# Pooling differences and low parts of weights spread over three stages of a decoder block, their loads held in place on the DMA queue

## The chip, the cores and the metric

The kernel runs on one core of one Trainium2 chip. The metric is the device time of one execution in microseconds (us). A core has five engines that work side by side: PE multiplies matrices (PEld are its weight loads), DVE and ACT work on whole tiles of 128 partitions, POOL too but only on SBUF, and SP here only issues DMAs. Each engine works off its instructions in an order fixed when the kernel is built; an instruction that waits holds back all behind it on its engine.

## The reference

One decoder block in float32, sequence and model width 1024, batch 1:

```python
h = rms_norm(x, norm_gain) * (1.0 + scale) + shift        # scale, shift, gate from silu(c) @ w_ada + b_ada
q, k, v, z_a, u, z_b, m_a, m_b = split(h @ w_in)          # eight parts of 1024 columns
attn = stick_breaking_attention(q, k, v)                  # 16 heads of 64
p_a = (attn * silu(z_a)) @ w_branch_a
pooled = multiscale_causal_pool(u, pool_w, pool_scale)
p_b = (pooled * silu(z_b)) @ w_branch_b
out = (sigmoid(m_a) * p_a + sigmoid(m_b) * p_b) @ w_out
return rms_norm(x + gate * out, final_gain)
```

The pooling has four groups of 256 channels with windows 2, 4, 8 and 16. For each group it takes the mean over the trailing window minus the token itself (the "difference"), maps it with a 256 x 256 matrix of the group, and scales each channel.

## The kernel before

To keep float32 accuracy, every operand of a large product is held as two halves: a high half (the value rounded to the type that PE takes) and a low half (the value minus the high half). A product is three matmuls: high by high, high by low, low by high. A weight tile is 128 x 1024 (512 KB). A step that projects with one tile has 2 x 24 = 48 matmuls of 512 columns. `split` makes the halves with a cast on one engine and a subtraction on another.

The work goes in stages, in this order of the program:

- u stage: h is made, and u = h @ w_in's part is written to DRAM (`u_d`), the last tiles in the loop `for i in reversed(range(KB))`.
- V stage (`with pool("vp")`): 16 steps of 24 matmuls; ACT and DVE make both halves of each output `vo`, and SP stores them to `v_d`.
- pooling stage (first half of `with pool("pb")`): for each of the four groups two differences are made from u on DVE (L384 to L399), the group's matrix is loaded and split (`praw`, `phl`), and for each of two steps j a projection with a `wzb` tile (48 matmuls) goes through silu into two tiles `zs`; then 12 pooling matmuls read the differences' halves `dhl`, and the scaled product goes to `gb` in halves.
- pb stage: eight steps of 48 matmuls multiply `gb` by `w_branch_b`; `gacc` and `bg` gather the gate.
- attention with the remaining projections ("p"), then the two last products and the norm.

The attention stage needs the low halves of 40 weight tiles. Eight it makes itself. The other 32 ("lows") are made ahead by `make_lo`: load a tile on SP (L134), cast on ACT (L136), subtract on DVE (L137), store to `wl_d` on SP (L138). Calls of it stand in the u stage (8), in V (`LO_V`, 14) and in pb (`LO_PB`, 10).

What sets the order: a planner orders the instructions of each engine when the kernel is built, by the order of the program and by when it expects their inputs and buffers. A DMA that has its buffer may be put far ahead of its place in the program. `tc.keep_in_program_order(ins)` ties an instruction behind the one traced before it on its engine; before the change that is used for loads of the first stage, and for PE's order there and in attention. Buffers with one tag are shared: weight tiles have two raw buffers (`raw`) and two of halves (`whl`), PE's outputs of projections have two banks (`pj`), those of pooling two (`tr`).

Of the kernel before, what the change touches and what calls it, by code (L numbers as in the profile page):

```python
# [9 lines left out]
F32 = mybir.dt.float32  # L10
F32R = mybir.dt.float32r
AF = mybir.ActivationFunctionType
ALU = mybir.AluOpType
PSUM = bass.MemoryType.PSUM

P = 128
D = 1024
S = 1024
# [16 lines left out]


PLAIN = 8
LO_V = (1, 1, 1, 1, 1, 1, 1, 0)
LO_PB = (1, 1, 1, 1, 1, 1, 2, 2)
HD = 64  # L40
BUSY = (10, 2, 2, 2, 6, 2, 0, 2)
EPS = 1e-6
WINDOWS = (2, 4, 8, 16)
# [5 lines left out]
def block_kernel(ctx, tc, a, out):  # L49
    nc = tc.nc  # L50
    v, act, gp = nc.vector, nc.scalar, nc.gpsimd

    def pool(name, **kw):
        return tc.tile_pool(name=name, bufs=1, reuse_waits="tile", **kw)
# [58 lines left out]
        else:  # L113
            v.tensor_copy(dst, src)

    def load_w(src, name, hi_eng, lo_eng):
        raw = wts.tile([P, KB, P], F32, tag="raw", bufs=2, name=name + "_raw")
        nc.sync.dma_start(raw.rearrange("p k c -> p (k c)"), src)
        return split(raw, [P, KB, P], wts, "whl", 2, hi_eng, lo_eng, name)


# [7 lines left out]
    def make_lo(pl, n):  # L129

        for _ in range(n):
            i = next(early_lo)
            raw = pl.tile([P, D], F32, tag="lraw", bufs=3, name=f"l{i}_raw")
            nc.sync.dma_start(raw, a["w_in"][tiles[i]])  # L134
            hi = pl.tile([P, D], F32R, tag="lhi", bufs=1, name=f"l{i}_hi")
            act.copy(hi, raw)  # L136
            v.tensor_sub(raw.bitcast(F32R), raw, hi.bitcast(F32))  # L137
            nc.sync.dma_start(wl_d[i], raw)  # L138

    def load_parts(i, name):  # L140
# [22 lines left out]
    def hmov(sh):  # L163
        return lambda m, kb: m[:, kb, sh * 512:sh * 512 + 512]

    def project(ct, name, use, he, le):
        whl = load_w(a["w_in"][ct], name, he, le)
        for sh in range(2):
            ps = bank("pj", f"{name}_{sh}")
            mm3(ps, whl, (h_hi, h_lo), range(KB), hmov(sh))  # L170
            use(sh, ps)
# [14 lines left out]


    early = ExitStack()
    first = early.enter_context(pool("first"))
    with pool("init") as init:  # L190
        sig = const.tile([P, 8], F32, name="csig")
        act.activation(sig, c_v, AF.Sigmoid)
# [143 lines left out]
            make_h(1, kb, v)  # L336


    with pool("vp") as vp:
        def load_wv(hf, k2):  # L340
            raw = wts.tile([P, 2, 512], F32, tag="raw", bufs=2, name=f"wv{hf}_{k2}_raw")
            nc.sync.dma_start(raw.rearrange("p k c -> p (k c)"), a["w_v"][hf, k2])
            return split(raw, [P, 2, 512], vp, "wv", 6, act, v, f"wv{hf}_{k2}")

        wv = [[load_wv(0, k2) for k2 in range(4)]]
        for i in reversed(range(KB)):
            ps = bank("pj", f"u{i}_1")
            mm3(ps, whl[i], h, range(KB), hmov(1))
            use[i](1, ps)
            make_lo(vp, 1)  # L350
        for hf in range(2):
            if hf == 0:
                wv.append([load_wv(1, k2) for k2 in range(4)])
            for sb in range(8):
                ss = slice(sb * P, (sb + 1) * P)
                ps = bank("pj", f"v{sb}_{hf}")
                for kb in range(KB):
                    hh, hl = h_hi[:, kb, ss], h_lo[:, kb, ss]
                    wh, wl = (w[:, kb % 2] for w in wv[hf][kb // 2])
                    for n, (l, w) in enumerate(((hh, wh), (hh, wl), (hl, wh))):  # L360
                        mm(ps, l, w, start=kb == 0 and n == 0, stop=kb == KB - 1 and n == 2)

                vo = vp.tile([P, 8, 2, HD], F32R, tag="vo", bufs=3, name=f"vo{sb}_{hf}")
                pv = ps.rearrange("p (h d) -> p h d", d=HD)
                act.copy(vo[:, :, 0], pv)
                v.tensor_sub(vo[:, :, 1], pv, vo[:, :, 0].bitcast(F32))
                nc.sync.dma_start(
                    v_d[4 * hf:4 * hf + 4, :, sb].rearrange("n p c -> p n c"),
                    vo.rearrange("p (n h) i d -> p n (h i d)", h=2).bitcast(F32),
                )  # L370
                make_lo(vp, LO_V[sb])
    early.close()


    with pool("pb") as pb:
        invn = pb.tile([P, 16], F32, name="invn")
        for j in range(16):
            gp.memset(invn[:, j:j + 1], 1.0 / (16 - j))
        gb = pb.tile([P, 2, KB, S], F32R, name="gb")
        for g, win in enumerate(WINDOWS):  # L380
            dhl = []
            for cb in range(2):
                j = 2 * g + cb
                u = pb.tile([P, S + 16], F32, tag="u", bufs=2, name=f"u{j}")  # L384
                v.memset(u[:, S:], 0.0)
                nc.sync.dma_start(u[:, :S], u_d[j])
                cur, n, step = u, S + 16, 1
                while step < win:
                    nxt = pb.tile([P, S + 16], F32, tag="win", bufs=2, name=f"win{j}_{step}")
                    n -= step  # L390
                    v.tensor_add(nxt[:, :n], cur[:, :n], cur[:, step:step + n])  # L391
                    cur, step = nxt, 2 * step
                t0 = S - win + 1
                d = pb.tile([P, S], F32, tag="win", bufs=2, name=f"d{j}")
                v.scalar_tensor_tensor(d[:, :t0], cur[:, :t0], 1.0 / win, u[:, :t0], ALU.mult, ALU.subtract)
                tl = pb.tile([P, 16], F32, tag="tl", bufs=2, name=f"tl{j}")
                v.tensor_mul(tl[:, :win - 1], cur[:, t0:S], invn[:, 16 - win + 1:])
                v.tensor_sub(d[:, t0:], tl[:, :win - 1], u[:, t0:S])
                dhl.append(split(d, [P, S], pb, "dhl", 3, v, v, f"dhl{j}"))  # L399
            praw = wts.tile([P, 2, 256], F32, tag="raw", bufs=2, name=f"praw{g}")  # L400
            nc.sync.dma_start(praw, a["pool_w"][g].rearrange("(k p) d -> p k d", p=P))
            ph, pl_ = split(praw, [P, 2, 256], pb, "phl", 1, v, v, f"phl{g}")
            for ob in range(2):
                j = 2 * g + ob
                zs = [pb.tile([P, 512], F32, tag="zs", bufs=3, name=f"zs{j}_{sh}") for sh in range(2)]

                def silu(sh, ps):
                    act.activation(zs[sh], ps, AF.Sigmoid)
                    v.tensor_mul(zs[sh], ps, zs[sh])  # L409

                project(CZB + j, f"wzb{j}", silu, v, gp)
                for sh in range(2):
                    sl = slice(sh * 512, sh * 512 + 512)
                    ps = bank("tr", f"pool{j}_{sh}")
                    for cb in range(2):
                        (dh, dl) = dhl[cb]
                        oc = slice(ob * P, ob * P + P)
                        for i, (w, m) in enumerate(((ph, dh), (ph, dl), (pl_, dh))):
                            mm(ps, w[:, cb, oc], m[:, sl], start=cb == 0 and i == 0, stop=cb == 1 and i == 2)
                    z = zs[sh]  # L420
                    v.scalar_tensor_tensor(z, ps, psc_v[:, j:j + 1], z, ALU.mult, ALU.mult)
                    act.copy(gb[:, 0, j, sl], z)
                    v.tensor_sub(gb[:, 1, j, sl], z, gb[:, 0, j, sl].bitcast(F32))
        gacc, bg = (pb.tile([P, S + 16], F32, tag="u", bufs=2, name=n)[:, :D] for n in ("gacc", "bg"))
        nc.sync.dma_start(bg, a["b_gate"].broadcast_to([P, D]))
        for j in range(KB):
            sm = [pb.tile([P, 512], F32, tag="zs", bufs=3, name=f"sm{j}_{sh}") for sh in range(2)]
            whl = load_w(a["w_branch_b"][j], f"wb{j}", v, gp)
            wg = wts.tile([P, D], F32, tag="raw", bufs=2, name=f"wg{j}")
            nc.sync.dma_start(wg, a["w_gate"][j * P:(j + 1) * P, :])  # L430
            if j == 0:
                v.tensor_scalar_mul(gacc, wg, sc[:, 0:1])
            else:
                v.scalar_tensor_tensor(gacc, wg, sc[:, j:j + 1], gacc, ALU.mult, ALU.add)
            for sh in range(2):
                ps = bank("pj", f"pb{j}_{sh}")
                mm3(ps, whl, (gb[:, 0], gb[:, 1]), range(KB), hmov(sh))
                act.copy(sm[sh], ps)
                nc.sync.dma_start(pb_d[j][:, sh * 512:sh * 512 + 512], sm[sh])
            make_lo(pb, LO_PB[j])  # L440

        for hf in range(2):
            sl = slice(hf * 512, hf * 512 + 512)
            ps = bank("z", f"gate{hf}")
            mm(ps, ones, gacc[:, sl], start=True, stop=True)
            v.tensor_add(bg[:, sl], ps, bg[:, sl])
        nc.sync.dma_start(g_d, bg[0:1, :])


    logits = ExitStack()  # L450
# [388 lines left out]
```

## Time and profile before

| what | value |
|---|---|
| median of 3 runs | 1255.46 us (1254.77 to 1256.27) |
| the profiled execution: own time, span | 1254.13 us, 1252.4 us |
| mean granted clock of PE | 0.991 |
| busy over the span: PE, DVE, ACT, POOL | 97%, 65%, 44%, 18% |
| PE's u products end, V's end, pooling's end, pb's end | 120.5, 207.6, 326.9, 414.8 us |

The profiled execution was recorded by the hardware profiler; its times are counted from the span's start. A granted clock of 1 is PE's full speed of 2.4 GHz, 0.5 is 1.2 GHz, and means of a stretch lie between.

### The profile page before, as it was taken

The page shows a single profiled execution, that of the slowest core. Times are in us where ns is not written, and L with a number is a line of the kernel's source. Part 1 is how long each engine was busy: PE and PEld are TensorE (multiplying, and loading weights), DVE is VectorE, ACT ScalarE, POOL GpSimd, SP SyncE. Part 2 cuts the span into 40 slices and gives each one's busy share as a digit, 9 for nine tenths or more (in the row PEclk, how much of TensorE's full clock was granted, in tenths as well). Part 3 has the DMA queues.
Part 4 walks back from the last instruction along what each step waited for, and adds up shares of the span by engine and source line. Part 5 has one row for each costly group of instructions (what it writes and reads, how often), then busy time and mean ns, then how long its engine had stood idle before and what let it go on. Part 6 is the DMA issues. An engine that isn't in the chain of part 4 may idle for free.

```text
span 1252.4 us, 16055 instructions
## 1 busy us (share of the span) xinstructions
PE 1217.4 (97%) x5744; PEld 1006.5 (80%) x5744; DVE 810.9 (65%) x1081; ACT 547.6 (44%) x1026; POOL 226.1 (18%) x373
## 2 busy tenths in 40 slices
PE   5999999899999999999999999999999999899997
PEld 4888888688888888888888888888888888688886
DVE  7633452999411178786878878687787854675653
ACT  4654331321101265565656556566665644331101
POOL 2100010111222342222323122222212310000001
PEclk9999999999999999999999999999999999899999
DMA  9658994753333411233323224231233246964512
GB/s 351 237 181 329 347 351 176 269 177 102 118 136 133 152 47 51 72 125 103 125 70 114 84 97 126 93 124 59 87 118 102 93 132 220 358 214 151 194 59 85
DMA packets 72946, 192.97 MB, mean 154 GB/s; under 512 B 7713, under 2 KB 21025, under 8 KB 70946
## 3 DMA queue, kind: packets, MB, share of 16 engines
q1 hardware_dynamic: 62098, 172.80, 39.9%
q10 hardware_dynamic: 10768, 19.14, 4.6%
q8 instruction: 45, 0.74, 0.2%
q14 instruction: 35, 0.29, 0.1%
HBM read 137.38 MB, written 50.34 MB: 150 GB/s over the span
## 4 chain that ended last, share of the span: by engine, by line
PE 71%; issue 10%; DVE 10%; DMA 4%; POOL 2%; ACT 1%; SPq 0%; POOLq 0%; DVEq 0%; ACTq 0%
PE p L90 24%; PE pb L90 7%; PE v L90 7%; PE pa L90 7%; PE o L90 6%; PE u L90 4%; PE z L90 4%; PE av L90 4%; PE wt L90 4%; PE ua L90 2%; DMA l_raw<-in_w_in 1%; DVE om L579 1%; DVE be L580 1%; DVE win L391 1%; POOL om L577 1%
## 5 line engine op out<-in xcount | busy, mean ns | idle before, releaser
L90 PE MATMUL p<-hT,w 128*128 128x512 f32 x1920 | 534.5, 399 | 0.0
L90 PEld LDWEIGHTS p<-hT,w 128*128 128x128 f32 x1920 | 341.5, 188 | 56.7 <-issue 0.5
L579 DVE TENSOR_TENSOR_SCAN om<-om 128x512 f32<-128x512 f32 (+7 forms) x128 | 175.2, 1368 | 51.8 <-POOL om L577 28.3
L572 ACT ACTIVATE om<-z 128x512 f32<-128x512 f32 (+2 forms) x192 | 94.3, 491 | 103.9 <-PE z L90 101.9
L599 DVE TENSOR_TENSOR wt<-wt,wt 128x512 fp32r<-128x512 f32 (+1 forms) x160 | 101.0, 632 | 47.5 <-ACT wt L598 46.2
L577 POOL TENSOR_SCALAR_AFFINE_SELECT om<-om 128x128 f32<-128x128 f32 x128 | 65.8, 514 | 328.3 <-ACT om L572 301.9
L598 ACT CAST wt<-wt 128x512 fp32r<-128x512 f32 (+1 forms) x160 | 87.3, 546 | 68.7 <-PE wt L90 64.6
L580 DVE TENSOR_TENSOR be<-be,om 128x511 f32<-128x511 f32 (+7 forms) x128 | 99.7, 779 | 10.5
L90 PE MATMUL pa<-ga,wa 128*128 128x512 f32 x384 | 92.6, 399 | 4.7 <-ACT m_sg L176 4.7
L90 PE MATMUL av<-wt,vv 128*128 128x512 f32 x320 | 94.4, 376 | 0.0
L90 PEld LDWEIGHTS wt<-ident,be 128*128 128x128 f32 x576 | 72.1, 140 | 27.5 <-DVE wt L599 3.2
L573 ACT ACTIVATE be<-z 128x512 f32<-128x512 f32 (+2 forms) x192 | 93.6, 488 | 0.0
L90 PE MATMUL wt<-ident,be 128*128 128x128 f32 x576 | 89.2, 273 | 3.8 <-DVE wt L599 3.8
L90 PE MATMUL wzb<-hT,wzb 128*128 128x512 f32 x384 | 91.9, 394 | 0.1
L90 PEld LDWEIGHTS pa<-ga,wa 128*128 128x128 f32 x384 | 73.5, 192 | 21.6 <-ACT m_sg L176 5.1
L90 PE MATMUL o<-wo,mhl 128*128 128x512 f32 (+1 forms) x408 | 89.8, 377 | 0.0
L90 PE MATMUL pb<-gb,wb 128*128 128x512 f32 x384 | 88.1, 391 | 0.0
L90 PE MATMUL v<-wv,hT 128*128 128x512 f32 x384 | 87.2, 389 | 0.0
L90 PEld LDWEIGHTS wzb<-hT,wzb 128*128 128x128 f32 x384 | 73.0, 190 | 16.5 <-DVE zs L409 0.7
L90 PEld LDWEIGHTS o<-wo,mhl 128*128 128x128 f32 x408 | 73.5, 188 | 14.4
L90 PEld LDWEIGHTS pb<-gb,wb 128*128 128x128 f32 x384 | 72.1, 188 | 15.8
L90 PEld LDWEIGHTS v<-wv,hT 128*128 128x128 f32 x384 | 72.1, 188 | 14.9
(119 smaller groups left out, 1461.9 us busy)
## 6 DMA issues: line engine op xcount, KB each, us to landing
w_raw<-in_w_in SPq DMA_DIRECT2D x40, 512.0 KB, 4.4
l_raw<-in_w_in SPq DMA_DIRECT2D x32, 512.0 KB, 5.5
wl_d<-l_raw SPq DMA_DIRECT2D x32, 512.0 KB, 5.1
w<-wl_d SPq DMA_DIRECT2D x32, 512.0 KB, 3.7
v_d<-vo SPq DMA_DIRECT2D x16, 512.0 KB, 5.2
vv<-v_d SPq DMA_DIRECT2D x8, 1024.0 KB, 5.9
wa_raw<-in_w_branch_a SPq DMA_DIRECT2D x16, 512.0 KB, 4.5
wa<-in_w_mod SPq DMA_DIRECT2D x7, 1024.0 KB, 7.9
```

Of the source, the lines that this page charges most:

```text
L90: ins = op(*args, **kw)
L391: v.tensor_add(nxt[:, :n], cur[:, :n], cur[:, step:step + n])
L572: act.activation(om[:, b0:b0 + n], zp[:, :n], AF.Sigmoid, scale=-0.125)
L573: act.activation(be[:, b0:b0 + n], zp[:, :n], AF.Sigmoid, scale=0.125)
L577: gp.affine_select(out=tl[:, :P], in_=tl[:, :P], pattern=[[1, P]], compare_op=ALU.is_gt, fill=fill, base=0, channel_multiplier=-1)
L579: v.tensor_tensor_scan(om[:, :W], om[:, :W], om[:, :W], 1.0, ALU.mult, ALU.min)
L580: v.tensor_mul(be[:, 1:W], be[:, 1:W], om[:, :W - 1])
L598: act.copy(wt[:, 0, :off], pt[:, :off])
L599: v.tensor_sub(wt[:, 1, :off], pt[:, :off], wt[:, 0, :off].bitcast(F32))
```

## The change

Three differences (tiles 0, 1 and 2) are made in the V stage, after its steps 1, 5 and 10 (counted from 0); the other five in the pooling stage, after the projections of steps 0, 2, 3, 4 and 5. The lows are spread: 8 in the u stage, 6 in V, 10 in pooling, 8 in pb. Loads of u, of lows and of the first `wzb` tile (now traced in V, behind step 13) are held behind the DMA traced before them on SP (`load_behind`). The halves of `wzb` are made by ACT and DVE instead of DVE and POOL. A low is cast and subtracted in two pieces of 512 columns with one buffer for the high half, and there are two raw buffers for lows instead of three. `zs` has two buffers instead of three, `dhl` four instead of three. The tiles of the first stage, and later those of the differences, lie on the right side of the memory; `gacc` and `bg` have places of their own; the small constants `invn` are set earlier.

```diff
-LO_V = (1, 1, 1, 1, 1, 1, 1, 0)
-LO_PB = (1, 1, 1, 1, 1, 1, 2, 2)
+LO_V = (0, 1, 0, 1, 0, 1, 0, 0)
+LO_PB = (1, 1, 1, 1, 1, 1, 1, 1)
+DIFFS = {1: 0, 5: 1, 10: 2}
+DIFFS_POOL = {0: 3, 2: 4, 3: 5, 4: 6, 5: 7}
+LO_POOL = (1, 1, 1, 1, 1, 1, 2, 2)
...
+    def load_behind(dst, src):
+        tc.keep_in_program_order(nc.sync.dma_start(dst, src))
...
-            raw = pl.tile([P, D], F32, tag="lraw", bufs=3, name=f"l{i}_raw")
-            nc.sync.dma_start(raw, a["w_in"][tiles[i]])
-            hi = pl.tile([P, D], F32R, tag="lhi", bufs=1, name=f"l{i}_hi")
-            act.copy(hi, raw)
-            v.tensor_sub(raw.bitcast(F32R), raw, hi.bitcast(F32))
+            raw = pl.tile([P, D], F32, tag="lraw", bufs=2, name=f"l{i}_raw")
+            load_behind(raw, a["w_in"][tiles[i]])
+            for hf in range(2):
+                part = raw[:, hf * 512:hf * 512 + 512]
+                hi = pl.tile([P, 512], F32R, tag="lhi", bufs=1, name=f"l{i}_hi{hf}")
+                act.copy(hi, part)
+                v.tensor_sub(part.bitcast(F32R), part, hi.bitcast(F32))
             nc.sync.dma_start(wl_d[i], raw)
...
-    first = early.enter_context(pool("first"))
+    first = early.enter_context(pool("first", side="right"))
...
+    def make_d(j):
+        win = WINDOWS[j // 2]
+        u = dif.tile([P, S + 16], F32, tag="u", bufs=2, name=f"u{j}")
+        v.memset(u[:, S:], 0.0)
+        load_behind(u[:, :S], u_d[j])
+        cur, n, step = u, S + 16, 1
+        while step < win:
+            nxt = dif.tile([P, S + 16], F32, tag="win", bufs=2, name=f"win{j}_{step}")
+            n -= step
+            v.tensor_add(nxt[:, :n], cur[:, :n], cur[:, step:step + n])
+            cur, step = nxt, 2 * step
+        t0 = S - win + 1
+        d = dif.tile([P, S], F32, tag="win", bufs=2, name=f"d{j}")
+        v.scalar_tensor_tensor(d[:, :t0], cur[:, :t0], 1.0 / win, u[:, :t0], ALU.mult, ALU.subtract)
+        tl = dif.tile([P, 16], F32, tag="tl", bufs=2, name=f"tl{j}")
+        v.tensor_mul(tl[:, :win - 1], cur[:, t0:S], invn[:, 16 - win + 1:])
+        v.tensor_sub(d[:, t0:], tl[:, :win - 1], u[:, t0:S])
+        dhls[j] = split(d, [P, S], dif, "dhl", 4, v, v, f"dhl{j}")
...
-                make_lo(vp, LO_V[sb])
-    early.close()
+                make_lo(lo, LO_V[sb])
+                if 8 * hf + sb == 13:
+                    wzb0 = load_w(a["w_in"][CZB], "wzb0", act, v, True)
+                if 8 * hf + sb in DIFFS:
+                    make_d(DIFFS[8 * hf + sb])
...
-                zs = [pb.tile([P, 512], F32, tag="zs", bufs=3, name=f"zs{j}_{sh}") for sh in range(2)]
+                zs = [pb.tile([P, 512], F32, tag="zs", bufs=2, name=f"zs{j}_{sh}") for sh in range(2)]
...
-                project(CZB + j, f"wzb{j}", silu, v, gp)
+                project(CZB + j, f"wzb{j}", silu, act, v, wzb0 if j == 0 else None)
+                if j in DIFFS_POOL:
+                    make_d(DIFFS_POOL[j])
...
+                make_lo(lo, LO_POOL[j])
+        diffs.close()
+        late = ctx_pb.enter_context(pool("late", side="right"))
+        gacc, bg = (late.tile([P, D], F32, name=n) for n in ("gacc", "bg"))
...
-            make_lo(pb, LO_PB[j])
+            make_lo(lo, LO_PB[j])
```

## Rows read from the trace of the kernel before

**Rows 1.** The page's first part: engine, busy us (share of span), instructions.

```profile
PE 1217.4 (97%) x5744; PEld 1006.5 (80%) x5744; DVE 810.9 (65%) x1081; ACT 547.6 (44%) x1026; POOL 226.1 (18%) x373
```

**Rows 2.** Windows: stretch, its length, busy us (instructions) by engine, clock, DMA share, GB/s.

```profile
core 0: us, PE busy (x) PEld busy (x) DVE busy (x) ACT busy (x) POOL busy (x), PEclk, DMA share, GB/s
120.50:207.60 87.10, 87.10 (x386) 72.14 (x385) 32.95 (x34) 26.97 (x34) 5.26 (x18) 1.00 0.81 287
207.60:326.90 119.30, 113.59 (x481) 92.07 (x480) 109.72 (x142) 28.57 (x41) 19.78 (x8) 0.97 0.55 185
220.00:240.00 20.00, 17.65 (x78) 14.13 (x76) 19.93 (x23) 4.72 (x5) 5.67 (x2) 1.00 0.81 275
240.00:260.00 20.00, 16.74 (x58) 13.09 (x59) 20.00 (x29) 8.17 (x11) 1.41 (x1) 0.83 0.73 239
280.00:300.00 20.00, 20.00 (x89) 16.45 (x88) 19.83 (x27) 3.04 (x5) 2.40 (x1) 1.00 0.30 106
326.90:414.80 87.90, 87.90 (x385) 72.11 (x384) 14.25 (x15) 11.02 (x18) 18.09 (x8) 1.00 0.37 129
```

**Rows 3.** PE's timeline in the pooling stage: start, us, form, count, idle before and releaser.

```profile
235.65 2.01 PE L90 MATMUL wzb<-hT,wzb 128*128 128x512 f32 x8
240.44 4.60 PE L90 MATMUL pool<-dhl,phl 128*128 128x512 f32 x12 [2.79 <-DVE u L385]
247.86 1.15 PE L90 MATMUL pool<-dhl,phl 128*128 128x512 f32 x2 [2.82 <-DVE phl L114]
...
271.27 2.89 PE L90 MATMUL pool<-dhl,phl 128*128 128x512 f32 x12
```

**Rows 4.** The chain of waits: start, us, what.

```profile
120.52 87.05 PE v L90 x384
```

**Rows 5.** DVE's groups in the pooling stage: busy, mean ns of one, idle before.

```profile
L105 DVE TENSOR_TENSOR dhl<-d,dhl 128x1024 fp32r<-128x1024 f32 x8 | 15.3, 1909 | 0.0
L137 DVE TENSOR_TENSOR l_raw<-l_raw,l_hi 128x1024 fp32r<-128x1024 f32 x10 | 12.1, 1214 | 0.8 <-ACT l_hi L136 0.8
...
L391 DVE TENSOR_TENSOR win<-win 128x1037 f32<-128x1037 f32 x6 | 10.2, 1700 | 0.1
L391 DVE TENSOR_TENSOR win<-u 128x1039 f32<-128x1039 f32 x8 | 9.9, 1234 | 0.1
...
L395 DVE SCALAR_TENSOR_TENSOR d<-win,u 128x1021 f32<-128x1021 f32 x2 | 4.7, 2325 | 0.0
L114 DVE CAST wzb<-wzb_raw 128x1024 fp32r<-128x1024 f32 x6 | 4.1, 685 | 0.0
```

**Rows 6.** POOL's groups in the pooling stage.

```profile
L105 POOL TENSOR_TENSOR wzb<-wzb_raw,wzb 128x1024 fp32r<-128x1024 f32 x6 | 16.2, 2696 | 103.7 <-DVE wzb L114 103.7
```

**Rows 7.** ACT's and DVE's groups in the V stage.

```profile
L136 ACT CAST l_hi<-l_raw 128x1024 fp32r<-128x1024 f32 x15 | 15.8, 1051 | 21.4 <-DMA l_raw<-in_w_in 18.5 <-DVE l_raw L137 1.3 <-DVE vo L366 1.2
L366 DVE TENSOR_TENSOR vo<-v,vo 128x512 fp32r<-128x512 f32 x15 | 10.3, 689 | 22.1 <-ACT vo L365 20.4 <-DMA praw<-in_pool_w 1.7
L365 ACT CAST vo<-v 128x512 fp32r<-128x512 f32 x16 | 9.4, 587 | 37.6 <-PE v L90 35.0 <-DMA l_raw<-in_w_in 2.6
...
L110 ACT CAST wv<-wv_raw 128x1024 fp32r<-128x1024 f32 x2 | 2.1, 1054 | 1.1 <-PE v L90 1.1
```

**Rows 8.** The timeline around V's end.

```profile
197.33 0.69 DVE L366 TENSOR_TENSOR vo<-v,vo 128x512 fp32r<-128x512 f32 x1 [4.75 <-ACT vo L365]
...
207.39 16.25 PE L90 MATMUL wzb<-hT,wzb 128*128 128x512 f32 x71
```

**Rows 9.** DMA issues from 60 to 420 us: count, KB each, median us to landing.

```profile
l_raw<-in_w_in SPq DMA_DIRECT2D x32, 512.0 KB, 5.5
...
wb_raw<-in_w_branch_b SPq DMA_DIRECT2D x8, 512.0 KB, 3.4
```

**Rows 10.** What SP's queue waited for: us in total, times, longest.

```profile
SPq L138 <- DVE l_raw L137: 46.2, 27, 3.8
```

More of the change, by code (lines that the diff above doesn't have):

```diff
@@ L114, in copy_to, with load_w @@
             v.tensor_copy(dst, src)
-    def load_w(src, name, hi_eng, lo_eng):
+    def load_behind(dst, src):
+        tc.keep_in_program_order(nc.sync.dma_start(dst, src))
+    def load_w(src, name, hi_eng, lo_eng, behind=False):
         raw = wts.tile([P, KB, P], F32, tag="raw", bufs=2, name=name + "_raw")
-        nc.sync.dma_start(raw.rearrange("p k c -> p (k c)"), src)
+        (load_behind if behind else nc.sync.dma_start)(raw.rearrange("p k c -> p (k c)"), src)
         return split(raw, [P, KB, P], wts, "whl", 2, hi_eng, lo_eng, name)
@@ L164, in hmov, with project @@
         return lambda m, kb: m[:, kb, sh * 512:sh * 512 + 512]
-    def project(ct, name, use, he, le):
-        whl = load_w(a["w_in"][ct], name, he, le)
+    def project(ct, name, use, he, le, whl=None):
+        if whl is None:
+            whl = load_w(a["w_in"][ct], name, he, le)
         for sh in range(2):
@@ L336, in block_kernel @@
             make_h(1, kb, v)
+    invn = const.tile([P, 16], F32, name="invn")
+    for j in range(16):
+        gp.memset(invn[:, j:j + 1], 1.0 / (16 - j))
+    dhls = {}
+    def make_d(j):
[16 more added lines that the diff above has]
+        dhls[j] = split(d, [P, S], dif, "dhl", 4, v, v, f"dhl{j}")
+    lows = ExitStack()
+    lo = lows.enter_context(pool("lo"))
     with pool("vp") as vp:
@@ L349, in block_kernel @@
             use[i](1, ps)
-            make_lo(vp, 1)
+            make_lo(lo, 1)
+        early.close()
+        diffs = ExitStack()
+        dif = diffs.enter_context(pool("dif", side="right"))
         for hf in range(2):
@@ L370, in block_kernel @@
                 )
-                make_lo(vp, LO_V[sb])
-    early.close()
[L375 to L378, printed above, removed]
+                make_lo(lo, LO_V[sb])
[3 more added lines that the diff above has]
+                    make_d(DIFFS[8 * hf + sb])
+    with ExitStack() as ctx_pb:
+        pb = ctx_pb.enter_context(pool("pb"))
         gb = pb.tile([P, 2, KB, S], F32R, name="gb")
         for g, win in enumerate(WINDOWS):
[L381 to L399, printed above, removed]
+            dhl = [dhls[2 * g], dhls[2 * g + 1]]
             praw = wts.tile([P, 2, 256], F32, tag="raw", bufs=2, name=f"praw{g}")
@@ L423, in block_kernel @@
                     v.tensor_sub(gb[:, 1, j, sl], z, gb[:, 0, j, sl].bitcast(F32))
-        gacc, bg = (pb.tile([P, S + 16], F32, tag="u", bufs=2, name=n)[:, :D] for n in ("gacc", "bg"))
+                make_lo(lo, LO_POOL[j])
+        diffs.close()
+        late = ctx_pb.enter_context(pool("late", side="right"))
+        gacc, bg = (late.tile([P, D], F32, name=n) for n in ("gacc", "bg"))
         nc.sync.dma_start(bg, a["b_gate"].broadcast_to([P, D]))
         for j in range(KB):
-            sm = [pb.tile([P, 512], F32, tag="zs", bufs=3, name=f"sm{j}_{sh}") for sh in range(2)]
+            sm = [pb.tile([P, 512], F32, tag="zs", bufs=2, name=f"sm{j}_{sh}") for sh in range(2)]
             whl = load_w(a["w_branch_b"][j], f"wb{j}", v, gp)
@@ L447, in block_kernel @@
         nc.sync.dma_start(g_d, bg[0:1, :])
+    lows.close()
     logits = ExitStack()
```

## Prediction

> **What bounds the kernel now.** The engine table at the head of the profile comes first: PE is busy for 97% of the span [rows 1], so a change on other engines pays only where PE waits or runs slowly. The windows by stage show where that is [rows 2]. In the V stage PE is busy for all of its 87.10 us. In the pooling stage (207.6 to 326.9 us) it is busy for 113.59 of 119.30 us, and DVE for 109.72, which makes DVE the suspect. Between 220 and 260 us DVE has no free time, PE is idle for 2.35 and 3.26 us and the granted clock of the second half falls to 0.83; from 280 to 300 DVE is as full (19.83 of 20) and PE has no idle time at all. So DVE's load alone is not fatal: what hurts is that too much comes at the start.
>
> The PE timeline shows the two stops [rows 3]: the pooling matmuls at 240.44 and 247.86 us wait for DVE, first for a chain that makes a difference, then for the halves of the pooling weights. After the first stop twelve pooling matmuls take 4.60 us; later twelve take 2.89.
>
> How much is there to win? The chain of waits has V's 384 matmuls in 87.05 us, 0.2267 us each [rows 4]. The pooling stage has 480 of the same length, 108.8 us, and lasts 119.3: 10.5 us are lost. Idle time is 5.7 of it, the slow clock most of the rest. The Trainium skill (Perfetto Trace Analysis, Identifying the Most-Contended Engine) says that busy time of matmuls is a bad measure of the distance to the roofline and that busy time of weight loads is a good one. By that measure the stage holds 92.07 us of weight loads where V holds 72.14 in 87.10 [rows 2], which would be 111.2 us of full speed and only 8.1 us to win. I keep the count, since a weight load's busy time does not separate fast and slow clock; the lower cap appears below as a rival.
>
> **The change part by part.** *Three differences go to V.* One costs DVE log2(window) additions of a whole tile, one scaled subtraction, one cast and one subtraction for the halves. A whole-tile operation of two inputs takes 1.23, a cast 0.69 [rows 5]. With windows 2, 2 and 4 that is 4.4 + 4.4 + 5.6 = 14.4 us off the pooling stage (the tails of at most 15 elements left out). V's DVE has room: 32.95 busy of 87.10, and it loses lows too (22 before V's end in the program, now 14). Their three loads of u come on SP; cost nothing, hidden by V's matmuls. If one lands late, DVE stands in front of V's output copies; that belongs to the rival on the other side.
>
> *POOL leaves the wzb halves.* POOL subtracted six tiles in this stage at 2.70 us each [rows 6]. In the same stretch some DVE operations are stretched: the means 1.909, 1.700 and 2.325 of three groups stand against 1.234 of the clean one [rows 5]. The excess is 8 x 0.675 + 6 x 0.466 + 2 x 1.09 = 10.4 us, which I take as returned. The casts go to ACT, 4.1 us off DVE; eight subtractions come on, 8 x 1.23 = 9.8. ACT takes 8 x 1.05 = 8.4 [rows 7] on top of 28.57 of 119.3.
>
> *Lows.* Before, those of the pb stage were free to load early, and ten of them ran in the pooling stage: 12.1 us of DVE [rows 5]. Now ten belong there, spread over eight steps, and eight follow in pb, where DVE is busy for 14.25 of 87.90 [rows 2]. In halves one costs 2 x 0.69 [rows 7] rather than 1.21: 1.6 more for ten. In pb, POOL still splits wb and may stretch their subtractions; 14.25 of 87.90 hides that. With one buffer for the high half, ACT and DVE alternate, which makes the latency 2 x (0.59 + 0.69) = 2.55 us.
>
> DVE's sum for the stage: 109.7 - 14.4 - 10.4 - 4.1 + 9.8 + 1.6 = 92.2 us in some 110. That is 84%, under the 99% at which PE had no idle time between 280 and 300. So most of the 10.5 us should come free. For stops that remain I take 1.0 us; the bounds are none and the 5.7 of now.
>
> *The new wait at the boundary.* Every held load stands behind the DMA traced before it on SP. In the thirteenth V step this makes one line: store of V's output, load of a low, its halves, store of the low, and only behind that store the load of wzb0. That step's DVE subtraction starts at 197.33 and ends at 198.02 [rows 8]. From there: landing of the low, halves 2.55, landing of wzb0, cast 1.05, subtraction 1.21 [rows 7, 5]. A load of that size lands in 3.4 us where the queue is quiet and in 5.5 where it is full [rows 9]. So both halves of wzb0 are there at 198.0 + 3.4 + 2.55 + 3.4 + 1.05 + 1.21 = 209.6 at best and at 213.8 at worst, and PE leaves V at 207.4 [rows 8], where it goes straight into 71 wzb matmuls now. The new stop is 2.2 to 6.4 us long. Behind that low's store SP also holds the loads of the pooling weights, so PE has little else to do. I take 3.0, near the quiet end, since little else moves then. After it the clock is slow, as after the stop at 240 us: 4.60 - 2.89 = 1.7 us.
>
> *The rest costs nothing.* Two zs buffers instead of three: a step has 48 wzb matmuls, 10.9 us, between one use and the next, against some 3 us of ACT and DVE. Two raw buffers for lows: the loads are paced now anyway. The other side of the memory, gacc and bg with places of their own, POOL's small memsets earlier: all are far from their use; without that cover each costs an operation of at most 1.2 us.
>
> Sum: 10.5 - 3.0 - 1.7 - 1.0 = 4.8 us less. Against the profiled execution's own 1254.13 that is 1249.3; the median of the runs shown, 1255.46, is 1.3 higher, which makes 1250.6, rounded to 1250.5.
>
> **The rivals.** *The boundary is hidden.* If PE finds the pooling matmuls or the next wzb at 207 us, 3.0 + 1.7 stay saved: a gain of 9.5, 1246.0. For it: DMAs that are not held run ahead, as the ten lows did. Against it: tiles behind wzb0 share its two raw buffers and two buffers of halves, and its step is first.
>
> *Nothing measurable.* At the busy landing the stop is 6.4 and 1.7 of clock, and with 1.0 of small stops 1.4 are left: 1254.0. It would end there too if weight loads, not matmuls, set PE's pace in this stage and the rest of its loss stayed. Against the first, SP moves little at V's end; against the second, the count of matmuls. The weight-load measure of the Trainium skill (same page and section) would give 8.1 - 4.7 - 1.0 = 2.4 us of gain, an estimate of 1253.1.
>
> *Slower.* A low's store on SP waits for DVE [rows 10], and the next held load now waits behind that store. In the u stage eight lows thus become one line of landing plus 2.55 each. ACT and DVE work in a fixed order; if that order counts on 3.4 us and landings take 5.5, each low is 2.1 later than its place, eight of them 16.8. The copies of u and V queued behind a waiting cast on ACT free PE's two banks, and PE stops when they are more than one step of 24 matmuls late, 5.4 us. So from the third low on it costs, at most 16.8 - 5.4 = 11.4 us; less the gain of 4.8 this is 6.6 slower, 1262.1. For it: in V ACT waited 18.5 us for landings of lows [rows 7], with three buffers. Against it: PE lost nothing in V then, the queue was fuller, and V's lows now start anew behind each store.
>
> **How the numbers follow.** The forecast gets 0.55, the hidden boundary 0.13, nothing measurable 0.18 (0.15 for late landings, 0.03 for the smaller cap), slower 0.14. The range from 1245.5 to 1258.0 takes in the first three with their bounds and the milder part of the fourth; the forecast's own range is 1247.5 to 1253.0. A difference under 0.2%, 2.5 us, is about what a measurement of this kernel cannot tell from no change. Faster by more: 0.13 and 0.51 of the forecast's 0.55, so 0.64; the same: 0.18 and 0.04, less a little for its bad end, 0.21; slower: 0.15.
>
> **What would show it.** Right: DVE under 95 us in the pooling stage, no POOL subtraction in it and no two-input DVE group above 1.3 us; PE without stops at its third step; one stop of about 3 us at V's end that ends with wzb0's halves and is followed by a slow clock; lows in pb. Wrong: PE idle in the u or V stage behind ACT or DVE (slower); wzb or pooling matmuls right at V's end (hidden); DVE still full with PE waiting for dhl.

## The result and the profile after

The changed kernel took 1259.21 us (median of 7 runs, 1256.71 to 1260.89). The kernel before, on the same chip, took 1255.32 (7 runs, 1254.76 to 1256.85). The ratio is 1.0026, 95% interval 1.0016 to 1.0036: slower by 3.9 us where 4.8 less were forecast, and outside the range. The profiled execution took 1258.37 us, 4.2 more than the one before; its span is 1256.4 us, which holds 4.0 of that. The page's engine table of the changed kernel, to be read against [rows 1]:

```profile
PE 1213.0 (97%) x5744; PEld 1004.0 (80%) x5744; DVE 809.6 (64%) x1113; ACT 560.0 (45%) x1066; POOL 205.3 (16%) x365
```

It tells nothing: every share is within two points of what it was. The windows by stage, against [rows 2] (stretch, length, busy us by engine, clock, DMA share, GB/s):

```profile
core 0: us, PE busy (x) PEld busy (x) DVE busy (x) ACT busy (x) POOL busy (x), PEclk, DMA share, GB/s
...
120.50:207.60 87.10, 81.89 (x355) 65.99 (x355) 39.18 (x60) 22.00 (x37) 0.00 (x0) 1.00 0.68 227
207.60:220.00 12.40, 6.75 (x30) 5.26 (x28) 2.77 (x4) 3.20 (x5) 0.00 (x0) 0.93 0.73 224
220.00:240.00 20.00, 19.68 (x77) 16.09 (x78) 16.91 (x23) 7.17 (x11) 0.00 (x0) 0.87 0.76 260
240.00:260.00 20.00, 20.00 (x90) 16.57 (x89) 19.93 (x31) 6.46 (x10) 0.00 (x0) 1.00 0.59 221
...
326.90:414.80 87.90, 87.90 (x389) 72.80 (x389) 26.23 (x33) 19.58 (x33) 19.13 (x8) 1.00 0.64 216
```

From 240 us on the pooling stage is what was promised: PE full at full clock, POOL without a subtraction of `wzb`. But V, which had not one idle PE microsecond before, now has 5.2 in the same 87.10, and in the 12.4 us from 207.6 on, in which V ends, PE is idle nearly half the time. PE's timeline says where (start, us, form, count, idle before and what ended it):

```profile
120.31 21.92 PE L95 MATMUL v<-wv,hT 128*128 128x512 f32 x96
142.43 5.73 PE L95 MATMUL v<-wv,hT 128*128 128x512 f32 x24 [0.19 <-DVE vo L407]
150.77 11.22 PE L95 MATMUL v<-wv,hT 128*128 128x512 f32 x48 [2.60 <-DVE vo L407]
162.79 10.16 PE L95 MATMUL v<-wv,hT 128*128 128x512 f32 x43 [0.81 <-DVE vo L407]
174.18 1.43 PE L95 MATMUL v<-wv,hT 128*128 128x512 f32 x5 [1.23 <-DVE wv L110]
175.99 38.36 PE L95 MATMUL v<-wv,hT 128*128 128x512 f32 x168 [0.38 <-DVE vo L407]
220.31 13.41 PE L95 MATMUL wzb<-hT,wzb 128*128 128x512 f32 x48 [5.97 <-ACT wzb L115]
...
236.28 11.04 PE L95 MATMUL wzb<-hT,wzb 128*128 128x512 f32 x48
```

V stops five times, four of them for `vo`, the copies that free PE's banks. Then comes one stop of 5.97 us for wzb0, and 48 matmuls at 13.41 us instead of 11.04. After that not one stop is left up to the end of pb. The account, from first matmul to first matmul (the timeline for the starts, [rows 3, 4] and the windows for before; the first wzb after 220.31, the first pb matmul at 331.64 in the chain):

| stretch | before | after | difference |
|---|---|---|---|
| V's start | 120.52 | 120.31 | -0.2 |
| V, 384 matmuls | 87.05 | 94.03 | +7.0 (5.2 idle, the rest in the pieces beside the stops) |
| stop at V's end | 0 | 5.97 | +6.0 |
| pooling, 480 matmuls | 119.3 | 111.33 | -8.0 (10.5 regained, 2.5 lost to the slow clock at its start) |
| pb, 384 matmuls | 87.9 | 87.05 | -0.9 |
| sum | | | +3.9 |

The chain of waits from 100 us on shows the cause in V (start, us, what; of its pieces only the loads of lows and one store are shown):

```profile
100.28 6.13 DMA l_raw<-in_w_in
109.61 5.74 DMA l_raw<-in_w_in
118.57 4.63 DMA l_raw<-in_w_in
126.40 4.93 DMA l_raw<-in_w_in
134.54 4.43 DMA l_raw<-in_w_in
142.22 6.47 DMA l_raw<-in_w_in
...
151.52 3.80 DMA wl_d<-l_raw
...
155.34 5.37 DMA l_raw<-in_w_in
```

The lows of the u stage stand in one line, each load behind the store of the low before. The last load shown, at 155.34 us, is that of V's first low; it waited until the store begun at 151.52 had landed, which gave it one of the two raw buffers. The first casts of the eight begin at 95.74, 106.48, 115.43, 123.27, 131.41, 139.05, 148.77 and 157.08 us in the timeline: 8.8 apart in the mean, where a landing of 5.5 and halves of 2.55, the prediction's figures, make 8.05. Before they began between 87.91 and 121.59. How one of them stops PE is seen at the stop of 2.60 us in the timeline of all engines:

```profile
148.77 0.62 ACT L146 CAST l_hi<-l_raw 128x512 fp32r<-128x512 f32 x1 [7.23 <-DMA l_raw<-in_w_in]
149.29 0.58 ACT L406 CAST vo<-v 128x512 fp32r<-128x512 f32 x1
...
150.03 0.68 DVE L407 TENSOR_TENSOR vo<-v,vo 128x512 fp32r<-128x512 f32 x1
...
150.77 1.45 PE L95 MATMUL v<-wv,hT 128*128 128x512 f32 x5 [2.60 <-DVE vo L407]
```

ACT waits 7.23 us with a cast of a low in its hands; the copy of V's finished output stands behind it; PE, which has two banks for its outputs, waits until DVE has taken the rest of it. At V's end the line is the one that was forecast, only longer:

```profile
204.13 0.69 DVE L407 TENSOR_TENSOR vo<-v,vo 128x512 fp32r<-128x512 f32 x1 [0.28 <-ACT vo L406]
...
205.31 1.41 SPq L122 DMA_DIRECT2D l_raw<-in_w_in  x1
...
210.91 0.62 ACT L146 CAST l_hi<-l_raw 128x512 fp32r<-128x512 f32 x1 [1.38 <-DMA l_raw<-in_w_in]
...
213.67 0.32 SPq L148 DMA_DIRECT2D wl_d<-l_raw  x1
214.04 0.42 SPq L122 DMA_DIRECT2D wzb_raw<-in_w_in  x1
...
219.22 1.04 ACT L115 CAST wzb<-wzb_raw 128x1024 fp32r<-128x1024 f32 x1 [4.25 <-DMA wzb_raw<-in_w_in]
```

### The profile page after: what moved, and what is told of

The parts are those of the page before. It is cut to its first block, busy times and chain, and to the rows that moved or that the text cites. A ratio compares the mean times of both kernels' runs of the same rounds, so it can differ in the third digit from the quotient of the medians.

```text
span 1256.4 us, 16108 instructions
## 1 busy us (share of the span) xinstructions
PE 1213.0 (97%) x5744; PEld 1004.0 (80%) x5744; DVE 809.6 (64%) x1113; ACT 560.0 (45%) x1066; POOL 205.3 (16%) x365
## 4 chain that ended last, share of the span: by engine, by line
PE 69%; issue 10%; DMA 7%; DVE 6%; POOL 3%; ACT 2%; SPq 0%; POOLq 0%; DVEq 0%; ACTq 0%
PE p L95 23%; PE wzb L95 7%; PE pb L95 7%; PE pa L95 7%; PE o L95 6%; DMA l_raw<-in_w_in 4%; PE z L95 4%; PE wt L95 4%; PE av L95 4%; PE ua L95 2%; PE v L95 2%; PE pool L95 2%; DVE om L609 2%; DVE be L610 2%; PE u L95 1%
## 5 line engine op out<-in xcount | busy, mean ns | idle before, releaser
L147 DVE TENSOR_TENSOR l_raw<-l_raw,l_hi 128x512 fp32r<-128x512 f32 x64 | 44.1, 689 | 112.2 <-ACT l_hi L146 112.1
L146 ACT CAST l_hi<-l_raw 128x512 fp32r<-128x512 f32 x64 | 39.8, 621 | 129.2 <-DMA l_raw<-in_w_in 107.7
L95 PE MATMUL av<-wt,vv 128*128 128x512 f32 x320 | 94.1, 375 | 0.0
```

Source lines behind the costliest of these rows:

```text
L95: ins = op(*args, **kw)
L146: act.copy(hi, part)
L147: v.tensor_sub(part.bitcast(F32R), part, hi.bitcast(F32))
```

## The experiments

The theory after this result: two lines of held loads lose the time, that of the u stage's lows in V (7.0 us) and that of wzb0 behind a low (6.0 and 2.5 of clock), and the two are separate. The rival: V's stops come from what was moved into V, not from the order of loads.

**Only the u stage's lows set free.** (`make_lo` got a third argument, `held`; with False its load is an ordinary one.)

```diff
-            make_lo(lo, 1)
+            make_lo(lo, 1, False)
```

> The loads of the eight lows of the u stage are not held; everything else is the changed kernel. Theory (the lows of the u stage form one line of landing, halves, store, next load, and ACT's copies of V's outputs stand behind their casts): V takes 87 to 88.5 us again instead of 94.0, the stop at V's end stays at 5 to 6 us with its slow clock, and the time falls by 5 to 7 us to 1252 to 1254. Rival (V's loss comes from the three differences on DVE there): V stays at 92 to 94 us and the time within 2 us of 1259.2.

Measured: 1251.56 us (1250.18 to 1252.81), ratio to the kernel before 0.9965 [0.9952, 0.9978]: 7.7 less than the changed kernel, a little more than expected. V has one stop of 0.83 us left, the boundary keeps its own:

```profile
132.45 76.45 PE L95 MATMUL v<-wv,hT 128*128 128x512 f32 x336 [0.83 <-DVE vo L407]
214.78 12.49 PE L95 MATMUL wzb<-hT,wzb 128*128 128x512 f32 x48 [5.87 <-ACT wzb L115]
```

**Only wzb0 traced ahead of the low of step 13.**

```diff
-                make_lo(lo, LO_V[sb])
                 if 8 * hf + sb == 13:
                     wzb0 = load_w(a["w_in"][CZB], "wzb0", act, v, True)
+                make_lo(lo, LO_V[sb])
```

> The load of the first wzb tile is traced, and held, ahead of the low of V's step 13 instead of behind it. Theory (that low's landing, halves and store make the line at V's end): the first wzb matmul follows V's last within 0.5 us at full clock, 6.0 + 2.5 us saved, 1250 to 1252; V stays at 92 to 94 us. Rival (the two raw buffers or the halves' buffers come free late): a stop of over 3 us stays and the time is above 1255.

Measured: 1250.71 us (1247.86 to 1254.88), 0.9962 [0.995, 0.9974]. The mirror image: no stop at the boundary, and V as long as before (94.1 us), with four of its stops left.

```profile
151.69 22.50 PE L95 MATMUL v<-wv,hT 128*128 128x512 f32 x91 [3.00 <-DVE vo L407]
...
214.38 11.15 PE L95 MATMUL wzb<-hT,wzb 128*128 128x512 f32 x48
```

**Both.**

> Both edits together. Theory: the two losses are apart from each other and add up: V in 87 to 88.5 us, no stop at its end, pooling in 109 to 110, 1243 to 1246, faster than the kernel before. Rival (one loss hides the other, as a late V gives wzb0 its time): 1248 or more.

Measured: 1243.13 us (1243.1 to 1246.4), 0.9904 [0.9888, 0.9921]: 12 us faster than before, 16 faster than the change. The two losses add up (7.7 and 8.5 alone, 16.1 together). The differences are still in V, and V runs without a stop, so what was moved there is not what stopped it. PE's timeline, then the window of the pooling stage:

```profile
120.58 87.20 PE L95 MATMUL v<-wv,hT 128*128 128x512 f32 x384
207.62 11.04 PE L95 MATMUL wzb<-hT,wzb 128*128 128x512 f32 x48
```

```profile
207.60:316.60 109.00, 109.00 (x482) 90.26 (x481) 90.14 (x129) 38.16 (x60) 4.28 (x2) 1.00 0.54 189
```

The pooling stage takes the 108.8 us of its matmuls and no more, with DVE at 90.14.

**Nothing held at all** (base: the changed kernel).

```diff
-        tc.keep_in_program_order(nc.sync.dma_start(dst, src))
+        nc.sync.dma_start(dst, src)
```

> No load of lows, of u or of wzb0 is held; the lists, the places in the program and the split of wzb stay as in the changed kernel. Theory: V keeps its 87 us and wzb0 is there in time, but lows run ahead of their places into V and the start of pooling, so that DVE or DMA stops PE there for 2 to 6 us: 1246 to 1252. Rival (holding is what keeps pooling clean): pooling loses 8 us or more as before the change, 1254 or more.

Measured: 1254.02 us (1250.92 to 1255.77), 0.9981 [0.9971, 0.9992]. Neither expectation holds as a whole: the pooling stage lost 3.2 us (112.0 for its 108.8), as the theory had it, but V, which was to stay clean, took 96.0 us (121.53 to 217.56), with stops for `vo` in other places, the longest

```profile
164.72 23.68 PE L95 MATMUL v<-wv,hT 128*128 128x512 f32 x96 [2.94 <-DVE vo L407]
```

So holding is not the fault as such; some of the held loads protect V. Which ones, the next two tell, on the kernel with both edits (1243.13).

**V's six lows not held.**

```diff
-                make_lo(lo, LO_V[sb])
+                make_lo(lo, LO_V[sb], False)
```

> The kernel with both edits (1243.1), but the six lows of V are not held either; loads of u and of wzb0 stay held, lows of pooling and pb too. Theory (a held low in V starts behind a store that PE paces, so its lateness cannot grow; a free one runs early and puts its casts ahead of V's copies): V 89 to 95 us, 1245 to 1251. Rival (in the run where nothing was held, V lost to the differences, not to the lows): V within 1 us of 87, 1242.5 to 1244.5.

Measured: 1250.7 us (1249.63 to 1252.28), 0.9958 [0.9943, 0.9973]. As the theory had it: V took 94.4 us, so holding V's lows is worth some 7 us. The longest stop:

```profile
151.41 12.78 PE L95 MATMUL v<-wv,hT 128*128 128x512 f32 x48 [3.85 <-DVE vo L407]
```

**The loads of u not held.**

```diff
-        load_behind(u[:, :S], u_d[j])
+        nc.sync.dma_start(u[:, :S], u_d[j])
```

> The kernel with both edits, but the loads of u for all differences are not held; all lows of V, pooling and pb stay held. Theory (the lows make the trouble): V within 2 us of 87 and the time 1243 to 1246. Rival (differences that run early stand on DVE ahead of V's copies): V 90 us or more, 1246 to 1251.

Measured: 1245.42 us (1244.39 to 1245.71), 0.9912 [0.9896, 0.9929]; V 88.7 us with stops of 0.33 and 0.54. The theory's numbers hold. Whether holding these loads is worth anything stays open: the trace is 2.4 us longer than that with both edits, but the ratio's interval overlaps that one's, [0.9888, 0.9921].

**How many held lows does it take in the u stage?** First four of the eight, then two (`make_lo(lo, 1, i >= 4)` and `i >= 6`; the loop counts down).

> Base is the kernel with both edits (1243.1). Here the last four of the eight lows of the u stage are not held and the first four are. Theory (lateness adds up along the line of held lows and PE pays only what exceeds one V step): four held lows are late by some 2 us each, 8 against 5.4 us of slack, so V costs 0 to 3 us and the time is 1243 to 1246. Rival (any held low in the u stage shifts the whole line behind it): V 93 us or more, 1248 to 1251.

Measured: a median of 1247.77 us, 0.993 [0.9912, 0.9949], but the profiled execution was 1243.34 and the others 1247.5 to 1248.4. V took 88.4 us in the trace, which is that of the fastest execution and does not explain the median: undecided.

> The kernel with both edits, but the first two of the u stage's eight lows are held. Theory (lateness adds up along the line, 2 us each, and PE has 5.4 us of slack): V within 1 us of 87, 1243 to 1244.5 in all runs. Rival (any held low there costs): V above 89 us, 1246 or more.

Measured: 1249.62 us (1248.9 to 1252.86), 0.9953 [0.9936, 0.997], and V 94.6. Two held lows cost nearly as much as eight, and PE stops at once:

```profile
127.47 5.74 PE L95 MATMUL v<-wv,hT 128*128 128x512 f32 x24 [1.23 <-ACT u_sg L194]
134.29 5.73 PE L95 MATMUL v<-wv,hT 128*128 128x512 f32 x24 [1.07 <-DVE vo L407]
140.18 16.61 PE L95 MATMUL v<-wv,hT 128*128 128x512 f32 x72 [0.16 <-DVE vo L407]
158.93 56.32 PE L95 MATMUL v<-wv,hT 128*128 128x512 f32 x240 [2.14 <-DVE vo L407]
```

That topples my law of sizes, lateness that adds up low by low until it passes 5.4 us. With both edits the first cast of a low began at 88.11 us, because its load was free to go out early; as soon as the first is held, it stands behind loads of `wv` that wait for buffers, and begins at 95.42. The seven that follow are all later than with both edits, held or not.

**The waiting taken off ACT and DVE.** The kernel with two held lows, but POOL makes the halves of the eight lows of the u stage.

```diff
-                act.copy(hi, part)
-                v.tensor_sub(part.bitcast(F32R), part, hi.bitcast(F32))
+                copy_to(gp if pool_halves else act, hi, part)
+                (gp if pool_halves else v).tensor_tensor(part.bitcast(F32R), part, hi.bitcast(F32), op=ALU.subtract)
...
-            make_lo(lo, 1, i >= 6)
+            make_lo(lo, 1, i >= 6, True)
```

> The kernel with two held lows (1249.62 us, V 94.6 us with stops of 1.23, 1.07, 0.16 and 2.14), but POOL makes the halves of the eight lows of the u stage, so that none of their casts stands on ACT and none of their subtractions on DVE; the loads stay as they were, two of them held. Theory: a held load costs time because a cast or a subtraction that waits for it stands on ACT or DVE ahead of the copies that free PE's banks. Then the three stops before 150 us (2.46 us and the slow clock behind each) go, V takes 87 to 91 us and the time is 1243.5 to 1247; the stop at 158.93, where DVE waited for a load of u, may stay. Rival: the held load costs through SP's queue alone, by making the loads and stores behind it late. Then V stays at 94 or more and the time at 1249 or more, and stops with DVE or ACT as releaser stay before 150 us. Price of POOL: some 1.2 us for each of four operations of a low, so a low takes landing plus about 5 us instead of 2.55, with two buffers; DVE may be stretched beside it, which V's free DVE hides in both theories.

Measured: 1251.81 us (1249.53 to 1252.7), 0.9968 [0.9957, 0.998], V 95.95. The theory's numbers were missed, and by the time and V's length the rival would have it; the place of the stops says otherwise. (The granted clock of the kernel with two held lows is 1.00 from 120.5 to 150 us, so the slow clock that the expectation counted behind the first three stops was not there to be won.) PE's timeline, then what ACT and DVE did (all engines):

```profile
120.22 27.36 PE L95 MATMUL v<-wv,hT 128*128 128x512 f32 x120
154.76 61.57 PE L95 MATMUL v<-wv,hT 128*128 128x512 f32 x264 [7.18 <-DVE vo L407]
```

```profile
143.39 0.62 POOL L117 TENSOR_SCALAR l_hi<-l_raw 128x512 fp32r<-128x512 f32 x1 [3.55 <-DMA l_raw<-in_w_in]
...
151.39 0.62 ACT L115 CAST l_hi<-l_raw 128x512 fp32r<-128x512 f32 x1 [14.06 <-DMA l_raw<-in_w_in]
...
153.29 1.07 ACT L406 CAST vo<-v 128x512 fp32r<-128x512 f32 x2
```

While POOL does the waiting (up to 3.55 us at a time in V) PE runs 120 matmuls without a stop where the kernel with two held lows stopped three times. The first low of V is still on ACT, and its load came out of the same line, which POOL makes longer still, at 147.16 us in the timeline: there ACT waits 14.06 us, two copies of V's output pile up behind it, and PE stops for 7.18. So both halves of the mechanism are seen: the line sets how late a low is, and the lateness cost nothing while POOL did the waiting and 7.18 us where ACT did it with copies behind. Taken off one engine, the loss went to the next low.

The last three look at the side that went well.

**POOL put back on the wzb halves** (on the kernel with both edits).

```diff
-                project(CZB + j, f"wzb{j}", silu, act, v, wzb0 if j == 0 else None)
+                project(CZB + j, f"wzb{j}", silu, v, gp, wzb0 if j == 0 else None)
```

(and wzb0's halves likewise)

> The kernel with both edits, but the halves of wzb are made by DVE (cast) and POOL (subtraction) again. Theory (DVE has room once differences and lows are spread): DVE's groups are stretched by some 10 us in sum, its busy time in pooling rises from about 90 to about 96 us, PE loses 0 to 2 us: 1243 to 1245.5. Rival (POOL leaving wzb is what freed pooling): PE waits for DVE in pooling as before, 3 us or more lost, 1246 or above.

Measured: 1248.32 us (1245.67 to 1250.76), 0.9935 [0.9919, 0.9952]: 5.2 more by the medians, 3.9 by the ratios, so the rival was nearer. In the trace, the slowest of the four, the pooling stage takes 113.6 us, 4.8 more. DVE's busy time in it is 96.4 us, as the theory had it; what it got wrong is that PE would hardly notice. DVE's casts of the differences, with POOL on the halves, then without; below them two of POOL's subtractions with the DVE operation that each holds up, from the timeline with POOL:

```profile
L119 DVE CAST dhl<-d 128x1024 fp32r<-128x1024 f32 x5 | 5.3, 1064 | 0.0
```

```profile
L119 DVE CAST dhl<-d 128x1024 fp32r<-128x1024 f32 x5 | 3.4, 685 | 0.0
```

```profile
254.62 2.79 POOL L110 TENSOR_TENSOR wzb<-wzb_raw,wzb 128x1024 fp32r<-128x1024 f32 x1 [11.43 <-DVE wzb L119]
255.06 0.69 DVE L433 TENSOR_TENSOR zs<-wzb,zs 128x512 f32<-128x512 f32 x1
...
255.66 2.84 DVE L110 TENSOR_TENSOR dhl<-d,dhl 128x1024 fp32r<-128x1024 f32 x1
...
268.73 3.42 POOL L110 TENSOR_TENSOR wzb<-wzb_raw,wzb 128x1024 fp32r<-128x1024 f32 x1 [11.32 <-DVE d L371]
...
271.08 1.63 DVE L119 CAST dhl<-d 128x1024 fp32r<-128x1024 f32 x1
```

The mean of 1064 ns hides two kinds: three of the five casts take 0.68 to 0.70 us, and two, which met a POOL subtraction, 1.63.

**The three differences of V made together after its last step.**

```diff
-DIFFS = {1: 0, 5: 1, 10: 2}
+DIFFS = {15: (0, 1, 2)}
...
-                    make_d(DIFFS[8 * hf + sb])
+                    for d_ in DIFFS[8 * hf + sb]:
+                        make_d(d_)
```

> The kernel with both edits, but the three differences of V are all made after V's last step. Theory (what hurt pooling was too much DVE work at its start): 14 us of differences stand there beside the low of step 0; the first pooling matmuls come 10.9 us after V's end, so PE waits 2 to 6 us for dhl or for DVE's copies, then runs slowly for 2: 1246 to 1251. Rival (the lows at the start were the trouble, not the differences): under 1245.

Measured: 1251.82 us (1251.14 to 1254.55), 0.9973 [0.9962, 0.9985]: 8.7 more, just above the range expected. V stays clean at 87.0, the pooling stage takes 118.1 us, and two stops of the sizes of [rows 3] are back, here both for DVE's work on `zs`, which stands in line with the differences:

```profile
235.49 4.60 PE L95 MATMUL pool<-dhl,phl 128*128 128x512 f32 x12 [2.75 <-DVE zs L448]
242.91 7.31 PE L95 MATMUL wzb<-hT,wzb 128*128 128x512 f32 x24 [2.82 <-DVE zs L434]
```

**The kernel before, with only the wzb halves on ACT and DVE.**

```diff
-                project(CZB + j, f"wzb{j}", silu, v, gp)
+                project(CZB + j, f"wzb{j}", silu, act, v)
```

> The kernel before with one edit: the halves of wzb are made by ACT and DVE. Theory (POOL's subtractions stretched DVE by 10.4 us in a stage that DVE paced, a third of it before 260 us): pooling 115 to 118 us instead of 119.3, 1251 to 1254. Rival (the start is crowded by differences and lows whoever splits wzb): within 1.5 us of the kernel before.

Measured: 1255.56 us (1255.08 to 1259.63), 0.9998 [0.9988, 1.0009]. Alone it gives nothing, as the rival had it: in the trace, the slowest of the ten, pooling lasts 119.9 us, and between 240 and 251 us PE still stops four times for DVE, for 6.4 us in sum (5.6 before). As long as differences and lows crowd the start of the stage, POOL's departure frees nothing that PE waits for.

## Why the prediction was wrong

**The pooling stage was right.** The 10.5 us were there and came back in full: 108.8 us from first to last matmul with both edits, no stop in the changed kernel from 220.31 us on. DVE was put at 92.2 us and measured 90.4 in the changed kernel. Both parts count: differences in V (8.7 us when they are put back at the stage's start) and POOL off the halves (some 4 to 5 us). The stops that were to remain, 1.0, were 0. The cap of 8.1 us worked out by busy time of weight loads (the Trainium skill, Perfetto Trace Analysis, Identifying the Most-Contended Engine) does not hold here, and the measurement decides: in the stage without stops they are busy for 90.26 us where they were for 92.07 [rows 2]. Part of that busy time belonged to the loss, since a weight load took 0.222 us in the mean at clock 0.83 and 0.186 at 1.00 (from 240 and from 220 us in [rows 2]).

**The step that failed: the overlap in V.** The prediction's sum has no term for V; the line of held lows, described with its place and mechanism, was kept as a rival, bounded at 11.4 us and given 0.14. It cost 7.0 us, and without it the kernel was faster than before (1251.56 with the u stage's lows free). What spoke against it did not hold. "PE lost nothing in V then" was true of lows free to load ahead, three buffers deep [rows 7]; held, ACT waited 42.9 us for them between 120.5 and 207.6 us where it had waited 18.5. The lighter queue took little off a landing: 5.0 us in the median in V against 5.7 before, at a DMA share of 0.68 against 0.81. "V's lows now start anew behind each store" held only from 176 us on, when the line was used up. That the line could not keep up follows from numbers on record, though no run varies its pace: in the u loop each low comes with 24 matmuls, 5.4 us of PE, and the line gives one in 8.8; in V one comes with two steps, 10.9 us, and there the line catches up.

**The stop at the boundary was right in kind, too small.** It stands where the prediction put it, wzb0 behind the store of a low, and 5.97 us lies inside the bounds of 2.2 to 6.4. The step that failed here is "near the quiet end, since little else moves then": the two loads took 5.52 and 5.15 us in the chain against 3.4 assumed. The window from 207.6 to 220 has a DMA share of 0.73; behind wzb0 went `praw`, a load of u and another low. Two smaller slips cancel: PE started right after the cast, without the subtraction's 1.21 us, and the links between the pieces, which were left out, took about 1.0. The slow clock after the stop cost 2.5 us where 1.7 was taken from a shorter one; in the run with only the u stage's lows free, behind a stop of 5.87, it cost 1.5, so its size is not settled by the stop's. Stop and clock were 4.7 in the sum and came to 8.5: with that alone the forecast would have been 1254.3.

**The rival's law of sizes was wrong too.** It let lateness grow by 2.1 us a low, forgave 5.4 and had PE pay from the third low on, in the u stage already; there PE lost nothing (V starts at 120.31 us, 120.52 before). Against the kernel with both edits two held lows cost 6.5 us by the medians, four 4.6 and eight 7.6. Shown is that the waiting low blocks the copies behind it on ACT (the kernel with POOL in its place), and that the first low already begins 7 us later. Whether four cost less than two is not settled by so few runs; why V lost only 1.4 us in the one execution traced with four is open: the order of ACT and DVE is planned anew for each kernel, and I did not find a number in the traces that gives it. Not run is the change with three raw buffers for lows instead of two; two alone cost nothing, as the kernel with both edits has them too.

**Sum by its own steps:** -10.5 + 6.0 + 2.5 + 7.0 and -1.1 at V's start and in pb make +3.9; forecast were -10.5 + 3.0 + 1.7 + 1.0.

## What to carry to other kernels

A load that is pinned behind a store waits for all that the store waits for; a row of such pairs is a line of round trips (8.8 us each here), and it costs wherever an engine in fixed order waits for it ahead of copies that the bound engine needs. Pin loads behind work that the bound engine paces, as V's six lows are (worth some 7 us), and trace what the next stage starts with ahead of helpers (8.5 us here). Leaving a row's first loads free to go out early belongs to it, but here only a row free as a whole was shown to be safe. If the same line is seen at two places in the profile, both are terms of the sum, not alternatives.

## What the runs showed of the hardware

Where POOL subtracts, DVE is not slowed down evenly. One operation whose operands all lie in SBUF is held up until POOL is done. In the kernel before, each of POOL's six subtractions in the pooling stage met one such operation, and all six ended 1.07 to 1.10 us after POOL's subtraction did. In two of the six DVE had begun another such operation just ahead, and there POOL took 3.3 us instead of 2.4. The "stretched" means of [rows 5] are means over these and over operations that met no subtraction and took their usual time. With POOL put back on the halves a cast, which has one input, is held up as well (1.63 us against 0.68), and a subtraction of three columns, 0.15 us elsewhere, took 2.35. Operations of DVE that read PE's output (`zs`) ran beside POOL at their usual 0.67 to 0.74 us. So in this kernel the price goes by the number of POOL's subtractions and by what DVE has next in its order.

A landing of 512 KB in V took 5.0 us in the median at a DMA share of 0.68 and 5.7 at 0.81. And a stop on PE costs more than itself: after 5.97 us the granted clock of the 20 us from 220 on was 0.87, and 48 matmuls took 13.41 us instead of 11.04; after 5.87 us in the run with only the u stage's lows free it was 0.93, and they took 12.49.
